# A hybrid decoder step on one core: a head's four normalised blocks turned into one PSUM bank and scaled by one operation

## The chip, the core and the metric

The kernel runs on one core of a Trainium2 chip. The core has a matrix engine (TensorE, PE in the profile; its weight loads are PEld), a vector engine (VectorE, DVE), an activation engine (ScalarE, ACT), a general engine (GpSimd, POOL) and a queue engine (SyncE, SP) that here only starts transfers. Matmuls write to PSUM, 128 partitions of eight banks, one bank holding 512 fp32 columns; DVE and ACT read PSUM and write SBUF. The metric is the device time of one execution in microseconds (us).

## What is computed

One layer of a decoder for a prompt of 512 tokens and for 32 decode tokens (8 sequences of 4): a half-step FFN, a mixing stage, a second half-step FFN. In the mixing stage four heads of differential attention and four heads of mLSTM (a matrix memory) run side by side on the same normalised input. The change touches the end of each head, where the output is normalised over its 128 columns and scaled by a gain per column:

```
attn = rmsnorm(attention(q_a, k_a, v_a), attn_norm) * (1 - lam_init)      # 4 heads x 128 columns
h_m, C, n, m = mlstm(q_m, k_m, v_m, gates)                                # 4 heads x 128 columns
h_m = rmsnorm(h_m, mlstm_norm) * sigmoid(o_m)
mixed = concatenate([attn, h_m], axis=-1)
return mixed @ w_out, ...
```

The attention is causal over the prompt; each head has two score maps, whose softmaxes are subtracted with a learned weight. The decode tokens also read a paged cache of 512 keys and values and a stored mLSTM state.

## The kernel before

Activations are kept with columns on the partitions and tokens along the free axis: `self.X` has eight blocks of 128 columns by 544 tokens (512 prompt, 32 decode). Every product with a weight matrix is three matmuls of a rounded high part and a remainder (lines 253 to 255), in two halves of 272 tokens. ACT rounds the weights (line 241) and DVE makes the remainder (line 242).

In the mixing stage the projections of w_in are the main stream on PE: for each half of each 128 columns 24 matmuls into a bank of the pool `acc` (three banks). DVE scales the result by the tokens' norms (lines 1224, 1225). Everything else is side work, written as Python generators that pause at each `yield`. After each half of a projection `side.step()` advances the queues by one step each: "prep" (turns keys and values, and brings in a head's attention blocks), "attn" (three places for blocks), "ml" (one mLSTM head), "mls" (the decode tokens' mLSTM), "smp" (the decode tokens' attention). A place is filled at the beginning of a step if it was free at the end of the step before. Counting steps from the first one behind the gates, the blocks of heads 0 to 3 begin to arrive in steps 1, 7, 11 and 15 (the first block in one step, the second in the next, the other two in the one after). The generators give the order in which the program is written; a planner that knows the dependencies and estimates durations then orders each engine's instructions, and each engine runs its list strictly in order. Buffers of one name rotate: a new one waits until the readers of the oldest are done. PSUM tiles from `ps_tile()` (name `aux`) rotate through three banks.

An attention block, `attn_block`, does 128 queries of one head: scores, bias and softmax (lines 1308 to 1332; a head's first block rounds the keys one step earlier), a pause of a step, transposes of the probabilities (1337, copied by ACT in 1339), the product with the values into a bank (1343), then the norm: ACT squares and sums into `y` (1346) and makes the factor (279, 280), DVE applies it (1348). Here the block pauses once more, and in its last step `head_out` turns `y` (128 tokens x 128 columns) on PE into a bank of its own (line 1245), and DVE scales it by the gain into `self.X` (line 1246). The decode tokens' mLSTM, `ml_sample_head`, only begins when no attention block has its scores still to do (lines 1569, 1570); its first transposes are line 1577.

An mLSTM head, `ml_head`, keeps its keys turned in `kt` (tokens on the partitions, four chunks of 128), then goes through the four chunks, one per step: state update `kv` from `kt` (line 1523), output `num` (1531, 1533), the norm (`ml_norm`, into `y` in lines 1481 and 1483), and `head_out` for the chunk before it. The last chunk's `head_out` follows the loop.

All these `y`, and the ones of the decode tokens, rotate through three buffers of 128 x 128. When the heads are done, `gated` multiplies the mLSTM blocks by the output gate (line 1814, for tokens 0 to 271 and then 272 to 511), `mixed` makes high part and remainder (1827, 1828), and the product with w_out follows on PE.

Of the kernel before, what the change touches and what calls it, by code (L numbers as in the profile page):

```python
# [19 lines left out]
SEQ = 512  # L20
NB = 8
NT = 4
NS = NB * NT
# [7 lines left out]
H = 4  # L31
# [174 lines left out]
class _Builder:  # L206
# [1031 lines left out]
            nc.tensor.transpose(ps[:, b * 128:b * 128 + 128], src[:, b * 128:b * 128 + 128], self.ident)  # L1238
        nc.scalar.copy(out=dst, in_=ps.rearrange("p (b d) -> p b d", b=4))

    def head_out(self, y, rows, which):

        nc = self.nc
        ps = self.ps_tile()
        nc.tensor.transpose(ps[:, 0:128], y, self.ident)
        nc.vector.tensor_scalar(out=rows, in0=ps[:, 0:128], scalar1=self.hg[:, which:which + 1], scalar2=None, op0=ALU.mult)


    def attn_head(self, h, k, v, side):
        nc = self.nc  # L1250
        hd = self.hd
        kt = hd.tile([128, 4, 128], F32, name="kt")
        vt = hd.tile([128, 4, 132], F32, name="vt")
        for qb in range(4):
            side.add("attn", self.attn_block(h, qb, self.X[:, 4 + h, :], k, vt))
            if qb < 2:
                yield
        self.tok_major(v, vt[:, :, 0:128])
        nc.gpsimd.dma_start(out=self.o["v_prompt"][0, 0].rearrange("(b p) h d -> p b h d", p=128)[:, :, h, :],
                            in_=vt[:, :, 0:128])  # L1260
        yield
        self.tok_major(k, kt)
        nc.gpsimd.dma_start(out=self.o["k_prompt"][0, 0].rearrange("(b p) h d -> p b h d", p=128)[:, :, h, :], in_=kt)
        nc.vector.tensor_copy(out=self.kas[:, h, :], in_=k[:, SEQ:T])
        nc.vector.tensor_copy(out=self.vas[:, h, :], in_=v[:, SEQ:T])
        self.new_keys += 1
# [28 lines left out]
                nc.vector.tensor_tensor(out=qt[rows, 2 + c, :], in0=q[own], in1=qt[own, c, :].bitcast(F32),  # L1295
                                        op=ALU.subtract)

    def attn_block(self, h, qb, q, k, vt):
        nc = self.nc
        wk = self.wk  # L1300
        n = (qb + 1) * 128
# [5 lines left out]
        z = wk.tile([128, 6], F32, name="z", bufs=6)  # L1307
        for c in range(2):
            ps = self.ps_tile()
# [25 lines left out]
        ps = self.ps_tile()  # L1335
# [6 lines left out]
        for kb in range(qb + 1):  # L1342
            nc.tensor.matmul(po[:, 0:128], lhsT=aT[:, kb * 128:kb * 128 + 128], rhs=vt[:, kb, 0:128],
                             start=kb == 0, stop=kb == qb)
        y = wk.tile([128, 128], F32, name="y", bufs=3)
        nc.scalar.activation(out=y, in_=po[:, 0:128], func=AF.Square, accum_out=z[:, 4:5])
        self.rstd_act(z[:, 4:5], DH, z[:, 4:5])
        nc.vector.tensor_scalar(out=y, in0=po[:, 0:128], scalar1=z[:, 4:5], scalar2=None, op0=ALU.mult)
        yield
        self.head_out(y, self.X[:, h, qb * 128:qb * 128 + 128], 0)  # L1350


    def attn_samples(self):
# [14 lines left out]
        for g in range(2):  # L1368
# [77 lines left out]
            for pg in range(NPG):  # L1446
# [6 lines left out]
                if g == 0:  # L1453
                    yield
                yield
            y = wk.tile([128, 128], F32, name="y", bufs=3)
            nc.vector.tensor_scalar(out=y, in0=po[:, 0:128], scalar1=dm[:, 0:1], scalar2=None, op0=ALU.mult)
            for h in range(1, H):
                nc.vector.scalar_tensor_tensor(out=y, in0=po[:, h * 128:h * 128 + 128], scalar=dm[:, h:h + 1], in1=y,  # L1459
                                               op0=ALU.mult, op1=ALU.add)  # L1460
            y2 = wk.tile([128, 128], F32, name="y", bufs=3)
            nc.scalar.activation(out=y2, in_=y, func=AF.Square, accum_out=z[:, 4:5])
            self.rstd_act(z[:, 4:5], DH, z[:, 4:5])
            nc.vector.tensor_scalar(out=y, in0=y, scalar1=z[:, 4:5], scalar2=None, op0=ALU.mult)
            yield
# [5 lines left out]
            yield  # L1471


    def ml_norm(self, num, den, e, n, z):

        nc = self.nc
        nc.scalar.activation(out=z[:, 0:1], in_=den, func=AF.Abs)
        nc.vector.tensor_tensor(out=z[:, 0:1], in0=z[:, 0:1], in1=e, op=ALU.max)
        nc.vector.reciprocal(out=z[:, 0:1], in_=z[:, 0:1])
        y = self.wk.tile([128, 128], F32, name="y", bufs=3)  # L1480
        nc.scalar.activation(out=y, in_=num, func=AF.Square, scale=z[:, 0:1], accum_out=z[:, 1:2])
        self.rstd_act(z[:, 1:2], DH, z[:, 1:2])
        nc.vector.tensor_scalar(out=y, in0=num, scalar1=z[:, 0:1], scalar2=z[:, 1:2], op0=ALU.mult, op1=ALU.mult)
        return y

    def ml_head(self, h, q, k, v):
        nc = self.nc
# [28 lines left out]
        nc.vector.tensor_tensor(out=pt, in0=ps.rearrange("p (c t) -> p c t", c=4), in1=E, op=ALU.mult)  # L1516
        yield
        C = None
        last = None
        for c in range(4):  # L1520
            s = slice(c * 128, c * 128 + 128)
            kv = self.ps_tile()
            nc.tensor.matmul(kv[:, 0:130], lhsT=kt[:, c, :], rhs=vt[:, c, 0:130], start=True, stop=True)
            Cn = wk.tile([128, 132], F32, name="C")
            if c == 0:
                nc.vector.tensor_copy(out=Cn[:, 0:130], in_=kv[:, 0:130])
            else:
                nc.vector.scalar_tensor_tensor(out=Cn[:, 0:130], in0=C[:, 0:130], scalar=fw[:, c:c + 1], in1=kv[:, 0:130],
                                               op0=ALU.mult, op1=ALU.add)
            num = self.ps_tile()  # L1530
            nc.tensor.matmul(num[:, 0:130], lhsT=pt[:, c, :], rhs=vt[:, c, 0:130], start=True, stop=c == 0)
            if c:
                nc.tensor.matmul(num[:, 0:130], lhsT=qw[:, s], rhs=C[:, 0:130], start=False, stop=True)
            z = wk.tile([128, 6], F32, name="z", bufs=6)
            y = self.ml_norm(num[:, 0:128], num[:, 128:129], self.ecol[:, c, h:h + 1], 128, z)
            if last:
                self.head_out(*last)
            last = (y, self.X[:, 4 + h, s], 1)
            C = Cn
            yield  # L1540
        self.head_out(*last)
        nc.gpsimd.dma_start(out=self.o["C_prompt"][0, 0, h], in_=C[:, 0:128])
        nc.vector.tensor_copy(out=self.nnew[:, NS + h:NS + h + 1], in_=C[:, 128:129])
        if h == H - 1:
            ps = self.ps_tile()
            nc.tensor.transpose(ps[0:H, 0:128], self.nnew[:, NS:NS + H], self.ident)
            nst = wk.tile([128, 128], F32, name="y", bufs=3)[0:H, :]
            nc.vector.tensor_copy(out=nst, in_=ps[0:H, 0:128])
            nc.gpsimd.dma_start(out=self.o["n_prompt"][0, 0], in_=nst)

# [83 lines left out]
    def ml_sample_end(self):  # L1634
        nc = self.nc
        z = self.wk.tile([128, 6], F32, name="z", bufs=6)
        y = self.ml_norm(self.nsb[:, 0:128], self.nsb[:, 128:129], self.ecs, 128, z)
        yield
        ps = self.ps_tile()
        nc.tensor.transpose(ps[:, 0:128], y, self.ident)  # L1640
        for h in range(H):
            for g in range(2):
                d = self.X[:, H + h, SEQ + 16 * g:SEQ + 16 * g + 16].rearrange("p (j t) -> p j t", j=4)
                nc.vector.tensor_scalar(out=d, in0=self.by_row(ps[:, 0:128], h, g), scalar1=self.hg[:, 1:2], scalar2=None,
                                        op0=ALU.mult)
        nc.tensor.transpose(ps[0:NS, 128:256], self.nnew[:, 0:NS], self.ident)
        nst = self.wk.tile([128, 128], F32, name="y", bufs=3)[0:NS, :]
        nc.vector.tensor_copy(out=nst, in_=ps[0:NS, 128:256])
        nc.gpsimd.dma_start(out=self.o["n_sample"][0].rearrange("b h d -> (b h) d"), in_=nst)

# [360 lines left out]
```

## Time and profile before

| What | Value |
|---|---|
| Times of three runs | 1103.85, 1106.62, 1107.76 us (median 1106.62) |
| Span of the profiled execution | 1109.2 us (no separate time of that execution is given) |
| Mean granted TensorE clock | 0.995 |
| Busy: PE, PEld, DVE, ACT, POOL | 1088.8, 1050.2, 855.4, 639.5, 163.2 us |
| Lines 1245 and 1246 | 32 instructions each, from 450.3 to 677.5 us |
| Line 1346 (attention's norm) | 16, from 444.4 to 587.9 us |
| Line 1481 (mLSTM's norm) | 17, first at 552.1 us |

The span runs from the first to the last instruction. In a list of groups a row has the line, engine, operation, result and operands by their program names, the shapes, the count, then the union of their busy time in us and the mean duration of one in ns, then the time that the engine sat idle just before them, with whatever ended it. In a list of waits a row has who waited, for whom, the total in us, how often, and the longest. A row of the timeline begins with the start in us and the busy time; brackets hold the idle time before it and what released it. In a table by window the columns are the stretch, its length, and the busy time of PE, PEld, DVE, ACT and POOL with their counts, then the granted clock, the transfers' share and GB/s. A row of one line's instructions has least, median and largest duration in ns, and the first and last start. Matmuls overlap, and their ends are modelled, so that busy PE time isn't time at full rate.

### The profile page before, as it was taken

The numbers are of one execution on the slowest core, as the hardware profiler recorded it, in microseconds if no ns is written. First come the engines' busy times: TensorE is split into PE (matmuls) and PEld (weight loads), VectorE is DVE, ScalarE is ACT, GpSimd is POOL, SyncE is SP. The second block draws the span as 40 slices with busy tenths as digits, with TensorE's granted clock in tenths as the row PEclk, the third lists the DMA queues.
The fourth block names the chain that finished last, engine by engine and source line by source line (L and its number), as shares of the span: only waits on it lengthen the run. The fifth ranks groups of instructions, "written<-read, shape, count | busy, mean of one in ns | idle before, by whom it ended". The sixth has DMA issues, their size and how long they took to land. (4 is left out here: it accounts for less than half of the span.)

```text
span 1109.2 us, 21539 instructions
## 1 busy us (share of the span) xinstructions
PE 1088.8 (98%) x8610; PEld 1050.2 (95%) x8610; DVE 855.4 (77%) x1626; ACT 639.5 (58%) x1288; POOL 163.2 (15%) x212
## 2 busy tenths in 40 slices
PE   9999999999999999999999999999999999999997
PEld 8999999999999998899789888999999999999997
DVE  5898787887677898668666477799978778957865
ACT  6554544565567756666545466675555455555664
POOL 3100000001210424320333442001000000012000
PEclk9999999999999999999999999999999999999999
DMA  9723233237994346533345545864223323299832
GB/s 265 252 94 114 81 111 115 76 96 208 223 245 128 93 121 172 175 112 82 103 148 160 178 136 177 248 216 161 89 87 105 114 77 106 67 270 206 191 97 81
DMA packets 145588, 160.33 MB, mean 145 GB/s; under 512 B 6013, under 2 KB 135397, under 8 KB 144208
## 3 DMA queue, kind: packets, MB, share of 16 engines
q1 hardware_dynamic: 115008, 99.05, 29.5%
q0 software_dynamic: 27472, 57.14, 20.8%
q10 hardware_dynamic: 3008, 2.78, 0.9%
q8 instruction: 67, 1.10, 0.4%
q14 instruction: 33, 0.27, 0.1%
HBM read 143.19 MB, written 16.28 MB: 144 GB/s over the span
## 5 line engine op out<-in xcount | busy, mean ns | idle before, releaser
L241 ACT CAST wh<-raw 128x512 fp32r<-128x512 f32 (+2 forms) x165 | 126.8, 795 | 97.3 <-PE acc L254 34.3
L242 DVE TENSOR_TENSOR wl<-raw,wh 128x512 fp32r<-128x512 f32 (+2 forms) x165 | 146.9, 904 | 43.4 <-ACT wh L241 42.7
L253 PE MATMUL acc<-h,wh 128*128 128x272 f32 x552 | 165.7, 300 | 0.0
L255 PE MATMUL acc<-h,wl 128*128 128x272 f32 x552 | 161.4, 293 | 0.0
L254 PE MATMUL acc<-h,wh 128*128 128x272 f32 x552 | 161.0, 292 | 0.0
L483 PE MATMUL acc<-t,wh 128*128 128x272 f32 x472 | 136.7, 290 | 0.0
L485 PE MATMUL acc<-t,wl 128*128 128x272 f32 x472 | 136.5, 290 | 0.0
L484 PE MATMUL acc<-t,wh 128*128 128x272 f32 x472 | 136.1, 289 | 0.0
L253 PEld LDWEIGHTS acc<-h,wh 128*128 128x128 f32 x552 | 104.9, 190 | 8.1 <-issue 7.5
L255 PEld LDWEIGHTS acc<-h,wl 128*128 128x128 f32 x552 | 104.9, 190 | 0.6 <-issue 0.4
L254 PEld LDWEIGHTS acc<-h,wh 128*128 128x128 f32 x552 | 105.1, 190 | 0.3 <-DVE y L1459 0.2
L483 PE MATMUL acc<-h,wh 128*128 128x272 f32 x360 | 104.2, 290 | 0.0
L485 PE MATMUL acc<-h,wl 128*128 128x272 f32 x360 | 104.2, 289 | 0.0
L484 PE MATMUL acc<-h,wh 128*128 128x272 f32 x360 | 103.6, 288 | 0.0
L242 DVE TENSOR_TENSOR wl<-X,wh 128x1024 fp32r<-128x1024 f32 x66 | 80.7, 1223 | 28.3 <-ACT wh L241 28.3
L241 ACT CAST wh<-X 128x1024 fp32r<-128x1024 f32 x66 | 69.3, 1050 | 40.6 <-PE aux L484 26.0
L484 PEld LDWEIGHTS acc<-t,wh 128*128 128x128 f32 x472 | 89.0, 189 | 0.0
L483 PEld LDWEIGHTS acc<-t,wh 128*128 128x128 f32 x472 | 88.8, 188 | 0.0
L485 PEld LDWEIGHTS acc<-t,wl 128*128 128x128 f32 x472 | 88.7, 188 | 0.1
L732 POOL DMA_DIRECT2D late<-in_ffn_w_down_dram x12 | 18.8, 1563 | 439.4 <-DVE wl L242 241.6
L485 PE MATMUL aux<-h,wl 128*128 128x272 f32 x240 | 69.6, 290 | 0.4 <-DVE wl L242 0.4
L483 PE MATMUL aux<-h,wh 128*128 128x272 f32 x240 | 69.4, 289 | 0.0
(522 smaller groups left out, 3288.6 us busy)
## 6 DMA issues: line engine op xcount, KB each, us to landing
raw<-in_ffn_w_gate_dram SPq DMA_DIRECT2D x18, 1024.0 KB, 5.8
raw<-in_w_in_dram SPq DMA_DIRECT2D x28, 512.0 KB, 4.8
late<-in_ffn_w_down_dram POOLq DMA_DIRECT2D x12, 1024.0 KB
rawx<-in_ffn_w_up_dram SPq DMA_DIRECT2D x10, 1024.0 KB
X<-in_ffn_w_up_dram SPq DMA_DIRECT2D x8, 1024.0 KB, 5.4
raw<-in_ffn_w_down_dram SPq DMA_DIRECT2D x8, 1024.0 KB, 8.6
raw<-in_ffn_w_down_dram SPq DMA_DIRECT2D x10, 768.0 KB, 4.5
raw<-in_w_out_dram SPq DMA_DIRECT2D x7, 1024.0 KB, 5.3
```

The costliest lines, as they stand in the source:

```text
L241: self.nc.scalar.copy(out=high, in_=src)
L242: self.nc.vector.tensor_tensor(out=low, in0=src, in1=high.bitcast(F32), op=ALU.subtract)
L253: nc.tensor.matmul(ps, lhsT=wh, rhs=xh(k0 + k), start=st, stop=False)
L254: nc.tensor.matmul(ps, lhsT=wh, rhs=xl(k0 + k), start=False, stop=False)
L255: self.last_mm = nc.tensor.matmul(ps, lhsT=wl, rhs=xh(k0 + k), start=False, stop=sp).ins
L483: nc.tensor.matmul(ps, lhsT=wh[:, k, cs], rhs=high, start=st, stop=False, skip_group_check=True)
L484: nc.tensor.matmul(ps, lhsT=wh[:, k, cs], rhs=low, start=False, stop=False, skip_group_check=True)
L485: self.last_mm = nc.tensor.matmul(ps, lhsT=wl[:, k, cs], rhs=high, start=False, stop=sp, skip_group_check=True).ins
L732: nc.gpsimd.dma_start(out=ts[j], in_=rows_of(a, j, up), accum_op=ALU.add)
```

## The change

The four outputs of a head stand in one tile and are turned together. For attention that is a new tile `ys` (128 x 4 x 128, one buffer), made by the head's first block; blocks 0 to 2 end with their norm, and block 3 pauses once more and turns all four. For the mLSTM the outputs go into `kt`, chunk by chunk, and one `head_out` follows the loop. The buffers named `y` are gone; the decode tokens' outputs and the small results use `an`, `aT`, `pw`, `sv` and `kt`.

```diff
-    def head_out(self, y, rows, which):
+    def head_out(self, ys, rows, which):
         nc = self.nc
         ps = self.ps_tile()
-        nc.tensor.transpose(ps[:, 0:128], y, self.ident)
-        nc.vector.tensor_scalar(out=rows, in0=ps[:, 0:128], scalar1=self.hg[:, which:which + 1], scalar2=None, op0=ALU.mult)
+        for b in range(4):
+            nc.tensor.transpose(ps[:, b * 128:b * 128 + 128], ys[:, b, :], self.ident)
+        nc.vector.tensor_scalar(out=rows, in0=ps, scalar1=self.hg[:, which:which + 1], scalar2=None, op0=ALU.mult)
...
     def attn_block(self, h, qb, q, k, vt, ys):
...
-        y = wk.tile([128, 128], F32, name="y", bufs=3)
+        if qb == 0:
+            ys.append(wk.tile([128, 4, 128], F32, name="ys", bufs=1))
+        y = ys[0][:, qb, :]
         nc.scalar.activation(out=y, in_=po[:, 0:128], func=AF.Square, accum_out=z[:, 4:5])
         self.rstd_act(z[:, 4:5], DH, z[:, 4:5])
         nc.vector.tensor_scalar(out=y, in0=po[:, 0:128], scalar1=z[:, 4:5], scalar2=None, op0=ALU.mult)
-        yield
-        self.head_out(y, self.X[:, h, qb * 128:qb * 128 + 128], 0)
+        if qb == 3:
+            yield
+            self.head_out(ys[0], self.X[:, h, 0:SEQ], 0)
...
     def attn_samples(self):
-            y = wk.tile([128, 128], F32, name="y", bufs=3)
+            y = an
...
-            y2 = wk.tile([128, 128], F32, name="y", bufs=3)
-            nc.scalar.activation(out=y2, in_=y, func=AF.Square, accum_out=z[:, 4:5])
+            nc.scalar.activation(out=aT[:, 0:128], in_=y, func=AF.Square, accum_out=z[:, 4:5])
...
     def ml_head(self, h, q, k, v):
-            y = self.ml_norm(num[:, 0:128], num[:, 128:129], self.ecol[:, c, h:h + 1], 128, z)
-            if last:
-                self.head_out(*last)
-            last = (y, self.X[:, 4 + h, s], 1)
+            self.ml_norm(num[:, 0:128], num[:, 128:129], self.ecol[:, c, h:h + 1], z, kt[:, c, :])
             C = Cn
             yield
-        self.head_out(*last)
+        self.head_out(kt, self.X[:, 4 + h, 0:SEQ], 1)
...
-            nst = wk.tile([128, 128], F32, name="y", bufs=3)[0:H, :]
+            nst = kt[0:H, 0, :]
...
     def ml_sample_end(self):
-        y = self.ml_norm(self.nsb[:, 0:128], self.nsb[:, 128:129], self.ecs, 128, z)
+        y = self.pw[:, 0:128]
+        self.ml_norm(self.nsb[:, 0:128], self.nsb[:, 128:129], self.ecs, z, y)
...
-        nst = self.wk.tile([128, 128], F32, name="y", bufs=3)[0:NS, :]
+        nst = self.sv[0:NS, 0:128]
```

More of the change, by code (lines that the diff above doesn't have):

```diff
@@ L1253, in attn_head @@
         vt = hd.tile([128, 4, 132], F32, name="vt")
+        ys = []
         for qb in range(4):
-            side.add("attn", self.attn_block(h, qb, self.X[:, 4 + h, :], k, vt))
+            side.add("attn", self.attn_block(h, qb, self.X[:, 4 + h, :], k, vt, ys))
             if qb < 2:
@@ L1296, in query_parts, with attn_block @@
                                         op=ALU.subtract)
-    def attn_block(self, h, qb, q, k, vt):
+    def attn_block(self, h, qb, q, k, vt, ys):
         nc = self.nc
@@ L1471, in attn_samples, with ml_norm @@
             yield
-    def ml_norm(self, num, den, e, n, z):
+    def ml_norm(self, num, den, e, z, y):
         nc = self.nc
@@ L1479, in ml_norm @@
         nc.vector.reciprocal(out=z[:, 0:1], in_=z[:, 0:1])
-        y = self.wk.tile([128, 128], F32, name="y", bufs=3)
         nc.scalar.activation(out=y, in_=num, func=AF.Square, scale=z[:, 0:1], accum_out=z[:, 1:2])
@@ L1483, in ml_norm @@
         nc.vector.tensor_scalar(out=y, in0=num, scalar1=z[:, 0:1], scalar2=z[:, 1:2], op0=ALU.mult, op1=ALU.mult)
-        return y
     def ml_head(self, h, q, k, v):
@@ L1518, in ml_head @@
         C = None
-        last = None
         for c in range(4):
```

## The prediction

> **What bounds the kernel now.** I read the page's busy times first, then the busy times by window over the mixing stage, then TensorE's waits, and last the timeline round the longest of them.
>
> ```profile
> span 1109.2 us, 21539 instructions
> ...
> PE 1088.8 (98%) x8610; PEld 1050.2 (95%) x8610; DVE 855.4 (77%) x1626; ACT 639.5 (58%) x1288; POOL 163.2 (15%) x212
> ```
>
> TensorE (PE) is busy for 98% of the span. Whatever leaves its work as it is can only win back the 20.4 us in which it is idle, and what a lowered clock costs. The change sits in the mixing stage, so the next view is that stage in windows.
>
> ```profile
> core 0: us, PE busy (x) PEld busy (x) DVE busy (x) ACT busy (x) POOL busy (x), PEclk, DMA share, GB/s
> ...
> 480.00:500.00 20.00, 19.29 (x151) 18.81 (x150) 15.95 (x63) 14.04 (x44) 1.91 (x3) 1.00 0.33 105
> 500.00:520.00 20.00, 19.36 (x153) 18.57 (x152) 16.22 (x64) 13.83 (x42) 2.50 (x4) 1.00 0.39 106
> ...
> 540.00:560.00 20.00, 18.66 (x138) 15.26 (x136) 16.53 (x68) 12.60 (x47) 6.10 (x6) 1.00 0.47 135
> 560.00:580.00 20.00, 18.23 (x140) 16.32 (x139) 11.61 (x48) 7.49 (x27) 10.06 (x13) 0.91 0.45 138
> ...
> 640.00:660.00 20.00, 20.00 (x205) 16.69 (x198) 14.67 (x56) 12.40 (x40) 5.45 (x8) 1.00 0.39 115
> ```
>
> Where attention runs (480 to 560), VectorE (DVE) is busy for four fifths and PE loses 0.6 to 1.3 us in 20; later (640 to 660) PE loses nothing. Who makes PE wait in this stage is in its list of waits; the three rows that name the operation which the change merges (line 1246, the scaling of a turned block) are these:
>
> ```profile
> PE aux L1523 <- DVE X L1246: 1.8, 1, 1.8
> ...
> PE aux L1311 <- DVE X L1246: 0.6, 1, 0.6
> ...
> PE aux L1493 <- DVE X L1246: 0.2, 1, 0.2
> ```
>
> Together 2.6 us in three places of 32. The longest, in order of time:
>
> ```profile
> 563.71 0.29 PE L255 MATMUL acc<-h,wl 128*128 128x272 f32 x1
> ...
> 564.64 0.37 PE L253 MATMUL acc<-h,wh 128*128 128x272 f32 x1
> 566.03 0.44 DVE L1224 TENSOR_TENSOR q<-acc,r 128x272 f32<-128x272 f32 x1 [2.43 <-PE acc L253]
> ...
> 566.39 0.60 DVE L1246 TENSOR_SCALAR X<-aux,hg 128x128 f32<-128x128 f32 x2
> 566.78 0.49 PE L1523 MATMUL aux<-vt,kt 128*128 128x130 f32 x2 [1.76 <-DVE X L1246]
> ```
>
> PE starts nothing between 564.64 and 566.78. It wants a PSUM bank for line 1523, and the scaling of two turned blocks, queued on DVE behind line 1224, holds what it waits for. But DVE itself had waited 2.43 us for PE before line 1224: the scaling ends this wait, and it is open whether it makes it. What follows the wait is in the clock:
>
> ```profile
> 428.00:431.00 3.00, 1.49 (x12) 1.27 (x10) 2.03 (x11) 2.81 (x9) 2.10 (x3) 1.00 0.71 181
> 431.00:436.00 5.00, 4.85 (x26) 4.50 (x26) 4.07 (x19) 3.29 (x12) 0.61 (x2) 0.66 0.56 174
> ...
> 564.00:567.00 3.00, 1.24 (x11) 1.03 (x9) 0.96 (x3) 0.76 (x4) 0.96 (x1) 1.00 0.75 232
> 567.00:572.00 5.00, 5.00 (x29) 4.96 (x29) 1.59 (x8) 1.23 (x6) 0.59 (x1) 0.66 0.05 17
> ```
>
> Twice PE was busy for only half of 3 us, and twice the granted clock of the next 5 us was 0.66: 5 x 0.34 = 1.7 us lost each time, while PE counts as busy.
>
> **The change part by part.** *TensorE's own work.* There are 32 transposes before (line 1245) and 32 after, eight groups of four. Nothing is removed.
>
> ```profile
> L1245 PE MATMUL aux<-base,y 128*128 128x128 f32 x32 | 8.3, 275 | 0.0
> ...
> L1238 PE MATMUL aux<-base,v 128*128 128x128 f32 x28 | 4.2, 272 | 0.0
> ```
>
> ```profile
> 561.21 0.27 PE L1245 MATMUL aux<-base,y 128*128 128x128 f32 x1
> ...
> 561.24 0.37 PE L254 MATMUL acc<-h,wh 128*128 128x272 f32 x1
> ```
>
> Line 1238 turns blocks four at a time: 4.2 / 28 = 0.15 us of PE time each, against 8.3 / 32 = 0.26 for the single ones. At most that is 32 x 0.11 = 3.5 us. I take 0, because a lone transpose's 0.27 us is not PE's alone: the matmul behind it starts 0.03 us after it. The 3.5 us are kept for the lower end of the range. Dearer than now they can't become: the same instructions on the same engine, only closer together.
>
> *VectorE.* Thirty-two scalings of 128 columns become eight of 512.
>
> ```profile
> L1246 DVE TENSOR_SCALAR X<-aux,hg 128x128 f32<-128x128 f32 x32 | 10.8, 345 | 2.8 <-PE aux L1245 2.6
> ...
> L1331 DVE SCALAR_TENSOR_TENSOR L<-L,z 128x512 f32<-128x512 f32 x4 | 3.0, 749 | 0.1
> ...
> L1516 DVE TENSOR_TENSOR L<-aux,L 128x512 f32<-128x512 f32 x4 | 2.7, 686 | 0.5 <-PE aux L1512 0.4
> ...
> L1330 DVE TENSOR_SCALAR L<-L,z 128x512 f32<-128x512 f32 x4 | 2.1, 529 | 0.1
> ...
> L1331 DVE SCALAR_TENSOR_TENSOR L<-L,z 128x128 f32<-128x128 f32 x3 | 1.1, 368 | 0.0
> ```
>
> The new form isn't in the trace. It lies between 529 ns (the same operation out of SBUF) and 749 (with a second tensor). Line 1331 grows by 749 - 368 = 381 ns from 128 to 512 columns, so I take 345 + 381 = 726, near the 686 of line 1516, which reads PSUM too. DVE: 32 x 345 = 11.0 us before, 8 x 726 = 5.8 after, 5.2 us less (4.9 to 6.9). DVE isn't the bound, so this counts only through PE's waits.
>
> *PSUM banks.* A transposed block took one of the three banks of that pool 32 times; now eight times, each held longer by three transposes and 0.38 us of scaling. With a quarter of the occasions I take a quarter of the three waits: 2.6 x 3/4 = 1.95 us less. The ends are 0 (another use of the banks waits in its place) and 2.6.
>
> *Clock.* If the 1.8 us wait is the one that goes, the 0.66 stretch behind it goes too: 1.7 us less; the ends are 0 and 1.7. The Trainium skill (TensorE: Matmul & The Clock Gate, section "Part 1: The HAM clock gate") has the clock halved after at least one idle window of about 3.4 us. The trace differs here: PE was idle for half of 3 us, no more, ahead of both stretches.
>
> *The order of the steps.* This the diff does without saying so. An attention block of rows 0 to 2 no longer pauses ahead of its transposition, so it leaves its place among the three active blocks one step earlier. A block stays five steps before (a head's first block six, because it rounds the keys first); after, blocks 0 to 2 stay four (the first one five) and block 3 five. Played through with three places and the heads arriving at steps 1, 7, 11 and 15, the last block of the last head computes its output in step 27 instead of 31, and the decode states, which wait until no block is left, start in step 24 instead of 28.
>
> ```profile
> L1348 DVE TENSOR_SCALAR y<-aux,z x16: 343/350/352, 445.5 to 588.9; 128x128 f32<-128x128 f32 x16
> ...
> L1577 PE MATMUL aux<-base,sm x8: 270/272/328, 574.6 to 677.9; 128*128 128x128 f32 x8
> ```
>
> The first of those outputs is step 5 (445.5) and the last step 31 (588.9): 5.5 us a step. So attention should end about 22 us earlier and the states' first transposes come about as much earlier. No work is added; it is packed more tightly. I take 0 for it; the end above is the slower rival's price.
>
> *New waits.* With one buffer for the four blocks, a head's first output on ScalarE (ACT) waits until the four transposes of the head before have read it. By the steps they come at the latest in the same step, ahead of it (heads 1 and 2). Queued behind it are ACT's weight roundings, for which DVE and then PE wait; a step of 5.5 us against four transposes of 0.15 hides it; uncovered it is 0.6 us, twice. In the mLSTM the outputs overwrite the key block that the matmul of line 1523 has just read, ahead of line 1531 on the same engine, whose result the output needs: no wait. The remaining edits only change which buffer a small result goes to, and each buffer has no later reader; I take 0 for them. The last mLSTM head is the case to watch, as its gating now waits for all four blocks.
>
> ```profile
> 674.88 0.35 DVE L1246 TENSOR_SCALAR X<-aux,hg 128x128 f32<-128x128 f32 x1 [0.97 <-PE aux L1245]
> 675.34 0.44 DVE L1814 TENSOR_TENSOR X<-X,q 128x272 f32<-128x272 f32 x1
> ...
> 677.51 0.35 DVE L1246 TENSOR_SCALAR X<-aux,hg 128x128 f32<-128x128 f32 x1
> ...
> 683.36 0.44 DVE L1828 TENSOR_TENSOR h<-X,h 128x272 fp32r<-128x272 f32 x1
> ```
>
> Before, its first half was gated at 675.34, after the third block. Now the one scaling has three more transposes ahead of it (0.15 us each, line 1238) and takes 0.73: 677.5 + 0.45 + 0.73 = 678.7. Gating, rounding and remainder behind it, taken at 0.44 each, end at 680.0. The last remainder was made only at 683.36, so 3.4 us of other work cover it. Without that cover it would cost up to 3.8 us (678.7 + 0.44 against 675.34).
>
> *Sum.* -1.95 - 1.7 = -3.65 us. The profiled execution goes from 1109.2 to 1105.6. Its span lies 2.6 us over the median of the three runs (1106.62) and over the slowest (1107.76); nothing else of its time is shown. I assume that the median run has the same wait: 1106.62 - 3.65 = 1103.0 us.
>
> **The rivals.** (1) *The wait comes back elsewhere.* DVE's own 2.43 us of waiting for PE speaks for it: then line 1246 only stood last in the chain, and the long wait with its slow stretch recurs. Only the two short waits shrink: 0.8 x 3/4 = 0.6, giving 1106.0.
>
> (2) *The slow clock isn't the wait's doing.* The wait goes, the 0.66 stretch stays: 1106.62 - 1.95 = 1104.7. For it: in 540 to 560 PE lost 1.34 us and the clock stayed at 1.00. Against it: both slow stretches stand right behind the two emptiest windows. By the section of the Trainium skill's page TensorE: Matmul & The Clock Gate named above, waits this short would not lower the clock; what this rival would show is just that.
>
> (3) *Slower: attention packed into fewer steps.* DVE has 16 of 20 us in the attention windows now. If its share of a step passes PE's, PE waits for line 1311's operands and for weight remainders. I price two more windows like 480 to 520 (0.7 us each) and one long wait with its slow stretch (1.8 + 1.7): 4.9, less 0.8 of the short waits, so 1110.7. It decides if DVE passes about 18 of 20 us in two windows running. Against it: blocks that start singly spread their bursts.
>
> (4) *It doesn't do what it says:* the key block is ordered as a whole, so each next chunk's line 1523 waits for the output before it. Twelve waits like line 1311's 0.6 us make 7.2, so 1113.8. A step of 5.5 us between chunks speaks against it.
>
> **How the numbers follow.** Forecast 0.42, (1) 0.18, (2) 0.17, (3) 0.20, (4) 0.03. A measurement of this kernel tells 0.3% (3.3 us) from no change, so (1) and (2) are "same": 0.35; (3) and (4) are "slower": 0.23; the forecast, 0.33% below, is just "faster": 0.42. Its own range is 1099.5 (with the 3.5 us of batched transposes) to 1104.7. Over all, 1099 to 1111 holds it but for (4) and the outer parts of the forecast and of (3).
>
> **What would show it.** Right: eight scalings near 726 ns, DVE busy about 5 us less, at most one PE wait behind the scaling, no granted clock under 1.00 after 440, attention's last output near 567, PE's busy time unchanged within 3.5 us. Wrong: a new PE wait of over 1.5 us in 440 to 580, a slow stretch in another place, DVE over 18 of 20 us there, or PE idle near 678 to 684.

## The result, and the profile after

The changed kernel takes 1111.61 us (median, 1109.23 to 1113.3) against 1104.82 (1102.56 to 1107.76) for the kernel before, measured beside it: a ratio of 1.0056, 95% interval 1.0041 to 1.0071. It is slower, by 0.41 to 0.71%, where the prediction said 1103.0 and faster. The profiled execution took 1111.6 us, its span 1109.8.

The head of the page of the changed kernel (its line numbers from here on: the four transposes are line 1246, the scaling 1247):

```profile
span 1109.8 us, 21518 instructions
## 1 busy us (share of the span) xinstructions
PE 1091.5 (98%) x8610; PEld 1050.7 (95%) x8610; DVE 853.9 (77%) x1602; ACT 638.5 (58%) x1288; POOL 163.6 (15%) x212
```

The busy times differ from those of before by 2.7 us at most (PE). The change did what it says, as rows of single lines in the changed kernel show (ns least/median/largest, then first and last start):

```profile
L1247 DVE TENSOR_SCALAR X<-aux,hg x8: 742/748/752, 475.7 to 677.5; 128x512 f32<-128x512 f32 x8
```

```profile
L1352 DVE TENSOR_SCALAR ys<-aux,z x16: 343/351/352, 444.2 to 572.9; 128x128 f32<-128x128 f32 x16
```

```profile
L1575 PE MATMUL aux<-base,sm x8: 272/272/273, 556.5 to 653.2; 128*128 128x128 f32 x8
```

Eight scalings of 0.75 us instead of 32 of 0.35; attention's last output at 572.9 instead of 588.9; and the decode states' first transposes at 556.5 instead of 574.6, the last head's at 653.2 instead of 677.9. That last row becomes the story.

The mixing stage by windows, changed kernel:

```profile
480.00:500.00 20.00, 18.89 (x133) 18.16 (x132) 17.06 (x65) 14.63 (x46) 1.59 (x2) 0.91 0.23 69
500.00:520.00 20.00, 19.48 (x148) 18.32 (x147) 16.43 (x63) 15.12 (x48) 2.04 (x3) 1.00 0.34 100
540.00:560.00 20.00, 20.00 (x135) 14.71 (x130) 12.26 (x45) 8.97 (x32) 9.87 (x12) 1.00 0.59 178
560.00:580.00 20.00, 19.48 (x155) 15.88 (x154) 13.07 (x44) 7.90 (x30) 6.41 (x9) 1.00 0.33 104
```

The hole of 1.8 us in 560 to 580 has gone, and the slow clock with it; a slow stretch stands behind 489 instead:

```profile
489.00:492.00 3.00, 1.89 (x13) 1.40 (x12) 2.68 (x9) 2.32 (x8) 0.80 (x1) 1.00 0.01 3
492.00:497.00 5.00, 5.00 (x32) 5.00 (x31) 4.27 (x18) 2.87 (x10) 0.00 (x0) 0.66 0.20 57
```

A second one stands near the start of the kernel, at 11 us, far from anything that the change touches. The same window of the kernel before comes last; it has 28 matmuls where the changed kernel has 16:

```profile
7.60:11.00 3.40, 3.27 (x19) 2.02 (x18) 2.89 (x6) 3.36 (x10) 1.24 (x3) 1.00 1.07 285
11.00:14.40 3.40, 3.40 (x16) 3.40 (x16) 2.83 (x7) 2.57 (x7) 0.00 (x0) 0.51 1.09 307
```

```profile
11.00:14.40 3.40, 3.40 (x28) 3.33 (x27) 2.96 (x6) 2.57 (x7) 0.00 (x0) 1.00 1.09 318
```

PE is busy for all of 540 to 560, and yet little gets through: 135 matmuls of all shapes, where the kernel with the state heads held back (below) has 149 in the same window:

```profile
540.00:560.00 20.00, 20.00 (x149) 17.31 (x147) 11.04 (x37) 7.85 (x31) 8.85 (x11) 1.00 0.60 185
```

A busy PE has to be read by what it does there. The list of PE's waits of the changed kernel from 640 to 720 (us in total, times, longest):

```profile
PE acc L255 <- DVE wl L242: 1.0, 1, 1.0
PE acc L253 <- ACT y L351: 0.6, 1, 0.6
PE smp L1454 <- DMA pgin<-in_cache_v_dram,idx: 0.6, 1, 0.6
```

The kernel before has no row at all in this stretch. The scaling is named neither here nor anywhere else from 420 to 720 any more. New are a wait for a weight's remainder, one for ACT and one for a page of cached values: line 1454, the decode tokens' value product. Its groups, first before and then after:

```profile
L1449 PE MATMUL smp<-pgin,saT 128*32 128x512 f32 x64 | 11.6, 601 | 0.1
```

```profile
L1454 PE MATMUL smp<-pgin,saT 128*32 128x512 f32 x64 | 13.6, 601 | 0.6 <-DMA pgin<-in_cache_v_dram,idx 0.6
```

The same 64 records of 601 ns each keep PE busy for 2.0 us longer. In the changed kernel's timeline:

```profile
551.42 1.04 PE L1454 MATMUL smp<-pgin,saT 128*32 128x512 f32 x2
552.40 0.73 PE L1313 MATMUL aux<-cs,vb 128*128 128x512 f32 x2
553.06 1.05 PE L1454 MATMUL smp<-pgin,saT 128*32 128x512 f32 x4
554.04 0.49 PE L1524 MATMUL aux<-vt,kt 128*128 128x130 f32 x2
554.46 1.04 PE L1454 MATMUL smp<-pgin,saT 128*32 128x512 f32 x2
...
566.68 1.06 PE L1454 MATMUL smp<-pgin,saT 128*32 128x512 f32 x8
567.68 0.40 PE L253 MATMUL acc<-h,wh 128*128 128x272 f32 x1
```

A page's value product is four matmuls (two records each), one per sequence, each on 32 columns of the array. At 566.68 the eight records are through in 1.00 us, side by side. At 551.42 the built order, which places each engine's instructions by estimates made beforehand, has other matmuls between them, and each of the three pieces takes 0.98 us: every cut costs one whole piece more. That such matmuls run at the same time is what the Trainium skill says (TensorE: Matmul & The Clock Gate, section "Part 3: Packing small matmuls — row/col tiling"); the trace agrees, with 1.00 us for eight records and 0.98 for two.

### The profile page after: what moved, and what is told of

It is laid out like the page before. It is cut to its first block, busy times and chain, and to the rows that moved or that the text cites. A ratio compares the mean times of both kernels' runs of the same rounds, so it can differ in the third digit from the quotient of the medians.

```text
span 1109.8 us, 21518 instructions
## 1 busy us (share of the span) xinstructions
PE 1091.5 (98%) x8610; PEld 1050.7 (95%) x8610; DVE 853.9 (77%) x1602; ACT 638.5 (58%) x1288; POOL 163.6 (15%) x212
## 4 chain that ended last, share of the span: by engine, by line
PE 81%; DVE 8%; ACT 5%; DMA 4%; issue 1%; POOL 0%; POOLq 0%; ACTq 0%; DVEq 0%; SPq 0%
PE acc L485 9%; PE acc L483 9%; PE acc L484 9%; PE acc L253 5%; PE acc L255 5%; PE acc L254 5%; PE aux L485 5%; PE aux L483 5%; PE aux L484 5%; PE smp L485 2%; PE smp L483 2%; PE smp L484 2%; ACT wh L241 2%; DVE wl L242 1%; DMA raw<-in_w_out_dram 1%
```

## The experiments

Each ratio is against the kernel before, run on the same chip. Four runs were made first, with two theories: the dropped pause (steps), or the merging itself.

**The kernel before, once more.** 

> The kernel before, unchanged, profiled a second time. The first profile has a span of 1109.2 us, and the changed kernel's has 1109.8 with a time of 1111.6, 1.8 more than its span; so the first profile belongs to an execution of about 1111, some 6 us over the median of 1104.8. If the two slow stretches at 431 and 567 us and the wait of 1.8 us are of that one execution, this profile has a span of about 1103 and neither of them; if they belong to the kernel, they stand here again and the span is near 1109.

1109.89 us. Its timeline, and the window behind the wait:

```profile
565.35 0.49 PE L1523 MATMUL aux<-vt,kt 128*128 128x130 f32 x2 [1.72 <-DVE X L1246]
```

```profile
567.00:572.00 5.00, 5.00 (x38) 3.74 (x37) 3.06 (x16) 2.29 (x7) 1.81 (x5) 1.00 0.15 28
```

The wait behind the scaling recurs, 1.72 us; the slow clock behind it does not, nor does the one at 431. The span, 1107.9, lies between the two that were expected: without the stretches it didn't fall to 1103.

**The pause kept, the rest as changed.**

```diff
-        if qb == 3:
-            yield
+        yield
+        if qb == 3:
             self.head_out(ys[0], self.X[:, h, 0:SEQ], 0)
```

> The change with one line moved back: blocks 0 to 2 keep the pause behind their norm, so the steps of attention and of all that waits for it are as before, and the merged transposes and scaling stay. Theory P (packing: the four steps by which attention ends earlier cost the time): 0.999 to 1.000 of before, 1103.7 to 1105. Theory M (merging: one bank and one operation for four blocks, or the outputs in the key tile, cost it): as the change, 1.005 to 1.006, about 1111.

1106.95 us, 0.9989 (0.9974 to 1.0004). All of the loss is gone with one step.

**The pause dropped, nothing merged** (kernel before).

```diff
-        yield
+        if qb == 3:
+            yield
         self.head_out(y, self.X[:, h, qb * 128:qb * 128 + 128], 0)
```

> The kernel before with the pause alone taken out of blocks 0 to 2: each turns and scales its own 128 columns at once, in the same step as its norm. Nothing is merged. Theory P: as the change, 1.004 to 1.006, 1109 to 1111.5. Theory M: 1.000, about 1105.

1113.34 us, 1.0050 (1.0034 to 1.0067): nearly the whole loss without any of the merge.

**Only the mLSTM heads merged** (kernel before).

```diff
-            y = self.ml_norm(num[:, 0:128], num[:, 128:129], self.ecol[:, c, h:h + 1], 128, z)
-            if last:
-                self.head_out(*last)
-            last = (y, self.X[:, 4 + h, s], 1)
+            self.ml_norm(num[:, 0:128], num[:, 128:129], self.ecol[:, c, h:h + 1], 128, z, kt[:, c, :])
...
-        self.head_out(*last)
+        self.head_out4(kt, self.X[:, 4 + h, 0:SEQ], 1)
```

> The kernel before with the mLSTM heads alone merged: their four outputs stay in the key tile, four transposes into one bank, one scaling of 512 columns behind the loop. Attention as before. Theory P: no change or a little less, 0.999 to 1.000. Theory M: part of the loss, 1.002 to 1.006, by how much of it sits in the mLSTM.

1106.97 us, 0.9990 (0.9978 to 1.0003). So the merge costs nothing that these runs can tell from zero, and the dropped pause costs nearly all. But how? It has two effects: attention's bursts stand closer, and the state heads start four steps earlier. By the steps the first group's value products fall in steps 22, 24, 26 and 28, the second's in 45 to 51; the four state heads start in steps 28, 34, 41 and 53 before, and in 24, 30, 36 and 45 after (the steps of the queue "ml" alone are counted too). So the first group now runs beside a state head from its second product on instead of at its last one, and the second begins with the last state head. As one head follows the other, the second group stands beside a state head either way. Four runs on that:

**The state heads held back.**

```diff
         while self.blocks_left:
             yield
+        for _ in range(4 if h == 0 else 0):
+            yield
```

> The changed kernel, with the first decode-state head held back four more steps, so that it starts where it started before the change; the attention blocks stay packed as the change packs them. Three theories of the 0.56% that the change costs. Collision: the loss comes from the state heads starting 16 to 22 us earlier, among the decode tokens' loads of value pages; then this run is back at 0.999 to 1.000 of the kernel before. Torn sets: four value matmuls on four column groups start 7 ns apart and run beside each other (a whole group of eight records took 0.97 to 1.00 us in all profiles), but where the built order puts other matmuls between them the group took 1.95; the built order has four such cuts in the changed kernel, two in the one with the pause kept, and it has three in this one and one cut score set fewer; so about 1.5 us are won and the ratio is about 1.0042. Density: attention's bursts themselves take the time, in places that neither of the two names; then the ratio stays at 1.005 to 1.006.

1105.43 us, 0.9988 (0.9976 to 1.0000); once more on another chip:

> The changed kernel with the state heads held back four steps, once more: 0.9988 as in its first run, 0.9975 to 1.000.

1107.67 us, 1.0011 (0.9991 to 1.0030). The loss is gone with attention as packed as in the changed kernel: density falls as a cause. The state heads' first and last transposes (line 1577 here), and the value product:

```profile
L1577 PE MATMUL aux<-base,sm x8: 270/272/328, 570.5 to 670.6; 128*128 128x128 f32 x8
```

```profile
L1454 PE MATMUL smp<-pgin,saT 128*32 128x512 f32 x64 | 11.6, 603 | 0.0
```

The list of waits of this run has no row at all from 640 to 720. Torn sets had 1.0042 for this run and were wrong: the order still cuts three sets here.

**The last page first** (changed kernel, all pages).

```diff
-                for j in range(4):
+                for j in (3, 2, 1, 0):
                     sj = slice(32 * j, 32 * j + 32)
                     nc.tensor.matmul(po[sj, :], lhsT=aT[:, pg * 128 + 32 * j:pg * 128 + 32 * j + 32], rhs=vps[j],
```

> The changed kernel, with the four value matmuls of a page taken from sequence 3 down to 0 instead of 0 up to 3; their sums are independent. The page of sequence 3 is asked for last, so when the first matmul of a set can start, the other three can too, and the built order holds one cut value set instead of four cuts. Torn sets: three cuts at 0.98 us each go, 2.9 us, so the ratio falls from 1.0056 to about 1.0030, and the value groups in the profile are again 0.97 to 1.00 us but for one. Collision and density: nothing that they name has changed, 1.005 to 1.006.

1109.33 us, 1.0023 (1.0009 to 1.0036). Three cuts fewer in the built order, and 0.33% of the time, 3.6 us, against 2.9 as priced. Cuts can be a part of this kernel's loss. The same edit with the pause kept, and in the kernel before:

> The changed kernel with the pause kept in every block (0.9989 in the run before) and the value matmuls from sequence 3 down to 0. The built order then has no cut value set instead of two. Torn sets: 1.96 us less than with the pause alone, a ratio of 0.997. The other theories: 0.999 as before.

> The kernel before, with nothing but the value matmuls from sequence 3 down to 0: the price of a cut by itself. Its built order has one value set in three pieces (2.93 us against 1.00 in its profile), and none with this edit. Torn sets: 1.95 us less, a ratio of 0.9982. The other theories: 1.000.

1112.83 us, 1.0056 (1.0039 to 1.0074), and 1108.11 us, 1.0005 (0.9986 to 1.0025). No theory had the first, and torn sets had neither. Both profiles have whole sets, and both wait for long for the last page, 4.7 and 3.3 us. Was that the turned order's doing, as the first matmul now waits for the page asked for last?

Four more: the heads held where the pause is dropped and nothing merged, the mirror image, the order turned in all pages but the last, and half the dose.

**The pause dropped, nothing merged, the heads held.** 

> The kernel before with the pause dropped in blocks 0 to 2 (that alone took 1.0050 of its time) and the first decode-state head held back four more steps, to step 28, where it stood before; nothing is merged. Collision: the earlier state heads are the whole cost of the dropped pause, so the ratio is back at 0.999 to 1.001. Torn sets: its built order has as many cut value sets as with the pause dropped alone (four cuts), so it stays at 1.004 to 1.006. Density: attention is packed as before, 1.005.

1108.93 us, 1.0010 (0.9992 to 1.0027): back, as collision had it. The value product, with the pause dropped alone and then with the heads held too:

```profile
L1450 PE MATMUL smp<-pgin,saT 128*32 128x512 f32 x64 | 12.4, 600 | 0.0
```

```profile
L1450 PE MATMUL smp<-pgin,saT 128*32 128x512 f32 x64 | 13.5, 602 | 0.2 <-DMA pgin<-in_cache_v_dram,idx 0.2
```

It takes 1.1 us longer in the faster kernel, nearly as long as in the changed kernel (13.6). So cut value sets are not what the early state heads cost here.

**The value products moved onto the state heads** (pause kept).

```diff
                 while self.new_keys < H:
                     yield
+                for _ in range(4):
+                    yield
```

> The mirror image: the changed kernel with the pause kept (0.9989), and the decode tokens' value products four steps later, so that in their first group they meet the first state head (step 28 against 26 to 32) as they do in the changed kernel (24 against 22 to 28), and in their second group the last one. Collision: as slow as the changed kernel, 1.003 to 1.006. Torn sets: three cuts instead of two, 1 us more, 1.000. Density: attention isn't touched, 0.999.

1111.57 us, 1.0042 (1.0026 to 1.0057). Attention is untouched, and the loss is there. Two rows of its timeline, at the third page of the second group:

```profile
677.03 2.15 PE L1456 MATMUL smp<-pgin,saT 128*32 128x512 f32 x6
679.75 1.04 PE L1456 MATMUL smp<-pgin,saT 128*32 128x512 f32 x2 [0.56 <-DMA pgin<-in_cache_v_dram,idx]
```

One product takes from 677.03 to 680.72 instead of 1.00 us, in pieces with a wait for a page between them. All value products together take 15.0 us, where they took 10.8 with the pause alone kept. One rival stays: the edit also moves the end of the decode tokens' attention, its last value product from 668.1 to 685.7.

**All pages but the last turned round** (pause kept). 

> The pause kept, and the value matmuls from sequence 3 down to 0 in all pages but the last of the second group, which keeps its order. In the run with all pages turned round the profile had whole sets (1.00 us each) and was 2.9 us ahead of the one with the pause alone at 640, and then waited 4.7 us for the last page, with a lowered clock behind it. If that wait is the order's doing (the first matmul of the set waits for the page asked for last), it shrinks here by the 0.95 us of the three matmuls that can go first, and the 2 us of the whole sets remain: 0.997. If the last page's arrival is a floor under the end of this stage, PE again comes too early and waits for it: 0.999 to 1.004, with a wait of over 2 us near 665.

1110.26 us, 1.0028 (1.0009 to 1.0047). The last product in its timeline, and the windows from there:

```profile
665.66 1.06 PE L1454 MATMUL smp<-pgin,saT 128*32 128x512 f32 x6
671.67 1.92 PE L1454 MATMUL smp<-pgin,saT 128*32 128x512 f32 x2 [4.96 <-DMA pgin<-in_cache_v_dram,idx]
```

```profile
660.00:668.00 8.00, 6.71 (x52) 4.84 (x51) 5.22 (x21) 6.03 (x25) 3.86 (x7) 1.00 0.72 224
668.00:676.00 8.00, 4.33 (x15) 2.58 (x16) 2.03 (x7) 1.03 (x5) 1.52 (x3) 0.57 0.31 104
```

The same kernel's queue of GpSimd had asked for that page here, behind the load of a state:

```profile
663.15 0.79 POOL L1557 DMA_DIRECT2D cs<-in_state_C_dram  x1 [1.84 <-DMA out_dram<-cs]
664.24 0.98 POOL L1365 DMA_INDIRECT pgin<-in_cache_v_dram,idx  x1 [0.30 <-issue]
```

In its list of transfers from 640 to 676:

```profile
pgin<-in_cache_v_dram,idx POOLq DMA_INDIRECT x9, 3.7
```

The other pages land in 3.7 us (median); this one kept PE waiting until 7.4 us after its request. The order within that set doesn't matter, since three of the four were through at once. In these runs the page's arrival is a floor under the end of this stage. The wait of 4.96 us is followed by a granted clock of 0.57 over 8 us, and 0.59 stands behind the 4.7 us of the first such run; in the profile of the second the clock stays at 1.00 behind its 3.3 us. That is where the runs with whole sets lost what they had won. A part of the lateness is on GpSimd's queue: the state load ahead of the page waits for a state's store, 1.84 us here and 1.89 in both other runs; with the pause alone kept and with the heads held it waits for no store, and GpSimd is idle for about 0.5 us at most ahead of it. Why the page then takes up to 7.4 us stays open.

**Held back two steps.** 

> The changed kernel with the first state head held back two steps instead of four: the dose. Collision: between the changed kernel's 1.0056 and the 0.9988 of four steps, 1.000 to 1.004, as the first value pages of the first group (asked for by step 26) no longer meet the state's loads in part. Torn sets: the built order has five cuts, one more than the changed kernel's four, so 1.006 or more.

1111.19 us, 1.0041 (1.0020 to 1.0062): just over collision's range, and under that of torn sets. Two steps don't undo it; the interval leaves open how much they undo.

What collides? Transfers (a state head moves 256 KB at a time on the queue that also brings the pages), or the order. Three runs side by side on one chip:

> The changed kernel once more, as the base for the two runs with fewer state transfers on the same chip. All theories: 1.0056 as before, 1.004 to 1.007.

1112.93 us, 1.0053 (1.0037 to 1.0069).

```diff
-                nc.gpsimd.dma_start(out=C[:, :, 0:128], in_=sC[4 * q2:4 * q2 + 4, h].rearrange("b d e -> d b e"))
+                nc.gpsimd.dma_start(out=C[:, 0:1, 0:128], in_=sC[4 * q2:4 * q2 + 1, h].rearrange("b d e -> d b e"))
...
-            nc.gpsimd.dma_start(out=oC[4 * q2:4 * q2 + 4, h].rearrange("b d e -> d b e"), in_=C[:, :, 0:128])
+            nc.gpsimd.dma_start(out=oC[4 * q2:4 * q2 + 1, h].rearrange("b d e -> d b e"), in_=C[:, 0:1, 0:128])
```

> The changed kernel with a quarter of the decode states' transfers: of each four states only the first is loaded and stored (64 KB instead of 256), and the products and updates of the other three read the first. What it leaves out: the other states' loads and stores, so the decode tokens' mLSTM is computed from the wrong states. The work of all engines and PE's built order stay as in the changed kernel. Transfers: the collision is gone, 0.998 to 1.000. Order: nothing changes that matters, 1.004 to 1.006.

> The same quarter of the state transfers, the same part left out, and the first state head held back four steps as in e4 (0.9988). The control: what fewer transfers are worth where the heads stand where they stood before. Transfers: within 0.1% of the run with the quarter alone. Order: 0.998 to 0.999, and 0.5% under the run with the quarter alone.

1112.05 us, 1.0052 (1.0038 to 1.0067), and 1106.20 us, 0.9997 (0.9983 to 1.0012). The transfers of the first, and its waits from 640 to 720:

```profile
cs<-in_state_C_dram POOLq DMA_DIRECT2D x8, 64.0 KB, 2.3
out_dram<-cs POOLq DMA_DIRECT2D x8, 64.0 KB, 2.4
```

```profile
PE acc L255 <- DVE wl L242: 1.0, 1, 1.0
PE smp L1454 <- DMA pgin<-in_cache_v_dram,idx: 0.4, 1, 0.4
```

A quarter of the bytes, and the loss and the two waits stand. The bytes aren't it; what is left is the order in which the engines and their queues do their work. As many transfers as before were issued (8 and 8), in the same places of GpSimd's queue, so these runs don't tell the order on that queue from the order on the engines. In the changed kernel the wait of 1.0 us looks like this, DVE first, then PE:

```profile
678.71 1.11 DVE L1622 SCALAR_TENSOR_TENSOR cs<-cs,sw,aux 128x128 f32<-128x128 f32 x4
...
681.00 1.30 DVE L242 TENSOR_TENSOR wl<-raw,wh 128x512 fp32r<-128x512 f32 x2
```

```profile
681.76 0.39 PE L255 MATMUL acc<-h,wl 128*128 128x272 f32 x1 [0.97 <-DVE wl L242]
```

The last state head's updates (line 1622) stand ahead of the remainder for w_out on DVE. With the heads held that line (1624 there) ends only later, behind this remainder:

```profile
L1624 DVE SCALAR_TENSOR_TENSOR cs<-cs,sw,aux x32: 325/340/348, 585.1 to 688.2; 128x128 f32<-128x128 f32 x32
```

**The price of a cut, and a better kernel.** The heads held and the first group's pages turned round, next to the held kernel on one chip:

```diff
-                for j in range(4):
+                for j in ((3, 2, 1, 0) if g == 0 else range(4)):
```

> The changed kernel with the state heads held back four steps (0.9988 in its first run), and the value matmuls from sequence 3 down to 0 in the first group only, so that its two cut sets are whole in the built order; the second group, with one cut, stays as it was. Price of a cut 0.98 us: two of them, 1.95 us, so 0.18% under the held run beside it, about 0.997 of the kernel before. If PE only comes earlier to the last page and waits for it there: no better than the held run, 0.998 to 1.000, with a wait for that page near 664.

1103.44 us, 0.9965 (0.9951 to 0.9979), against 1107.67 and 1.0011 for the held kernel beside it. The value product in the held kernel and then in this one:

```profile
L1454 PE MATMUL smp<-pgin,saT 128*32 128x512 f32 x64 | 11.7, 603 | 0.0
```

```profile
L1454 PE MATMUL smp<-pgin,saT 128*32 128x512 f32 x64 | 9.7, 601 | 0.0
```

Two cuts fewer, 2.0 us of PE time, no long wait for the last page: on PE the price of 0.98 us is shown. The medians differ by more, 4.2 us; the clock does part of it (mean granted clock 0.9978 against 0.9959 over the twelve executions each, some 2 us). Against the held kernel's first run, 0.9988, it is 0.23%, near the 0.18% that were expected. This kernel keeps the merge and the dropped pause and is faster than both kernels of this case.

## Why the prediction was wrong, point by point

**The step that failed** is the order of the steps: "No work is added; it is packed more tightly. I take 0 for it". The steps themselves were right (states from step 24 instead of 28; attention's end 16 us earlier instead of 22), and the prediction even named the state transposes that move. It stopped at attention and did not ask whom the states meet when they come earlier. That earlier start costs about 4 to 7 us: shown by holding the heads (1.0056 to 0.9988 and 1.0011; without the merge 1.0050 to 1.0010). That they meet the value products is shown from the other side, by moving these onto them (0.9989 to 1.0042), with the one rival named there.

**Where the loss lies** is shown. The main stream on PE (lines 253 to 255 into `acc`) is the same in all these kernels, so the start of one and the same matmul can be compared between two profiles. How far the kernel with the early state heads is behind the one with the heads held, in us, at three matmuls that the held kernel starts at 532, 589 and 691:

| Profiles | 532 | 589 | 691 |
|---|---|---|---|
| changed kernel and held kernel, first | 2.4 | 7.0 | 7.6 |
| the same two, second | 2.2 | 7.1 | 7.7 |
| the same with a quarter of the state transfers | -0.2 | 4.2 | 4.8 |
| pause dropped, nothing merged: without and with the heads held | 0.9 | 4.1 | 4.7 |

Between the first and the last it grows by 3.8 to 5.5 us in all four pairs, at a granted clock of 1.00, and most of that comes by 589, in the stretch where the first state head runs beside the first value group. A part of the growth by 589 may be state work that the held kernel still has ahead of it; but the lag isn't won back later.

**What it is made of** is shown only in part, and it isn't the same in each pair. The profiled spans of the changed kernel and the held one, 1109.8 and 1102.9, are 6.9 us apart. PE is busy for 5.5 us more, and 3.4 of them are the two slow stretches, at 11 and at 492, about 1.7 each. Both profiles of the changed kernel have them and neither of the held one's; but they come ahead of the state heads, and over all executions the clock doesn't tell the kernels apart (mean granted clock 0.9972 and 0.9973 in the two sets of the changed kernel, 0.9975 and 0.9959 in the held one's). Another 2.0 us are the value product (13.6 against 11.6: one cut more, and the last page's product broken by a wait). PE is idle for 1.4 us more: the held run has none of the waits for a remainder (1.0), for the last page (0.6), for ACT's line 351 (0.6) and of line 1532 near 560 (0.5), but others of its own. Without the merge the value product goes the other way (12.4 us, and 13.5 with the heads held), and what takes the time there stays open. That PE pays 0.98 us for a cut is shown by runs; that the waits come from the order on the queues is read from the timeline only.

**The three waits behind the scaling, -1.95.** They went in the changed kernel, and in the run with only the mLSTM merged the long one did. That run is 0.9990, about 1.1 us less than before: smaller than the term, and not told from zero.

**The clock, -1.7.** Wrong as a gain. The profile after shows no slow stretch at 567, but the kernel before, run once more, has the same wait of 1.72 us and the full clock behind it. So the slow stretch doesn't follow the wait each time, and rival (2) had this point right in part. In the changed kernel it is the same: PE is busy for 1.89 us of the 3 ahead of the slow stretch at 492 in both profiles, and for 1.90 in the run with a quarter of the transfers, where the clock stays at 1.00 and the kernel is as slow. The page of the Trainium skill that the prediction weighed there (TensorE: Matmul & The Clock Gate, section "Part 1: The HAM clock gate") has the clock judged over windows that run freely; if so, the same wait can fall on either side, and these executions agree with that. That a whole idle window is needed doesn't agree: PE was busy for 1.89 us of the 3 ahead of the slow stretch at 492, and for 3.27 of the 3.4 ahead of the one at 11.

**The profiled execution and the median.** "I assume that the median run has the same wait": the wait recurs, but its slow stretch doesn't. Time and span differ by about 2 us in these runs (1111.6 and 1109.8 here), so a span of 1109.2 is an execution of about 1111 (an estimate), well above the median of 1106.62. The 1.7 were subtracted from a median of which nothing shows that it holds them: the first profile's mean granted clock is 0.995, the second's, without these stretches, 0.998, and the mean over the 23 executions beside the second 0.9973. The stretches don't explain all of the distance, as the second profile's span is still 1107.9.

**VectorE.** Right for the operation: 748 ns against 726, so the scalings take 6.0 us instead of 10.8. (The prediction's bounds of 4.9 and 6.9 for the saving come to 5.0 and 6.8 from its own rows.) DVE as a whole is busy for only 1.5 us less, where about 5 were named as a sign; where the rest went wasn't followed. No gain from it shows in the time.

**New waits and the last head.** No wait of PE for the single buffer of four blocks shows. In the mLSTM, where none was expected, PE waits once for the norm's last operation (line 1486, into `kt`), ahead of line 1532 near 560, for 0.5 us; the held run has no such wait. The last scaling starts at 677.5 and ends at 678.2, where 678.7 was forecast. But PE does stand idle between 678 and 684, one of the signs named for a wrong prediction: at 681.76 it waits for the remainder of a weight, and the state head's updates are among what DVE does ahead of it, which the prediction had not put there.

**The rivals.** Rival (3) had the right edit (packing), the right sign and nearly the time (1110.7), by the wrong mechanism: DVE never passed 17.1 of 20 us between 480 and 600, and attention's density costs nothing by itself that the held runs can tell from zero. Rival (1) and rival (4) didn't happen.

## What to carry to other kernels

A step dropped from a queue of side work moves everything that waits for that queue: list what starts earlier, and what it will then stand beside. Where a build places instructions by its own estimates, a set of matmuls that run side by side costs PE a whole piece more for each cut. Taking first the one whose operand comes last keeps it whole, and that paid where the operand was there in time; where it was not, PE only waited. And a slow stretch in one profile is a property of that execution until others show it: the changed kernel had the same two in both its profiles, and their loss was still not the loss that the times show.

## What the runs showed of the hardware

Eight records of four 32-column matmuls take 1.00 us together, and two of them alone 0.98. A wait of 1.7 us was followed by a granted clock of 0.66 over 5 us in one execution and by 1.00 in another of the same kernel; a wait of 4.96 us by 0.57 over 8 us. Near the start the clock was 0.51 over 3.4 us in the changed kernel, behind 3.4 us in which PE was busy for 3.27, and 1.00 in the kernel before, behind 3.26. One page out of nine took 7.4 us until PE could go on, where the median was 3.7; its request stood behind a state load that had waited 1.84 us for a store, and what else held it wasn't found.
